# A decoder block on one core: the same program with its buffers at other places in SBUF

## The chip, the core and the metric

The kernel runs on one core of a Trainium2 chip. The core has TensorE (matrix products; called PE in the profile, its weight loads PEld), VectorE (DVE), ScalarE (ACT), GpSimd (POOL) and SyncE (SP), which issues the DMAs. They share an on-chip memory, SBUF, of 128 partitions; a buffer has the same byte range in every partition, and "place" below means the first byte of that range. Matrix products are written to another memory, PSUM. The metric is the time of one execution on the device in microseconds, the median over three executions.

## What is computed

One block of a decoder for 512 tokens of 1,024 features, in float32, with two attention branches and a feed-forward:

```python
xn = rmsnorm(x, norm_mix_g)
proj = xn @ w_in             # q_lat 384, kv_lat 256, k_rope 32, dq 512, dk 512, dv 512, gates 2048
# branch A: latent attention, 8 heads: q, k, v up-projected from the normed latents, rotary part shared by the heads
# branch B: differential attention, 4 heads: (softmax(q1 k1^T) - lam * softmax(q2 k2^T)) v, RMS norm per head
merged = sigmoid(g_mla) * (o_mla @ w_branch_mla) + sigmoid(g_diff) * (o_diff @ w_branch_diff)
x = x + merged @ w_out
hn = rmsnorm(x, norm_ffn_g)
hid = silu(hn @ w_ffn_gate) * (hn @ w_ffn_up)        # 2816 wide
x = x + hid @ w_ffn_down
return rmsnorm(x, norm_final_g)
```

## The kernel before

Every float32 operand of a product is split into a high and a low part (type float32r, `split` and `weights`), and `mm3` multiplies high by high, high by low and low by high into one PSUM bank: three matmuls, recorded on lines 297, 298 and 299. In the profile a matmul stands as `ps_mm<-X,w`: behind the arrow the first name is the operand that streams through TensorE, the second the stationary one, loaded ahead by a LDWEIGHTS. "128*128 128x512 f32" means 128x128 weights and 512 streamed columns, 2,048 bytes a partition.

The buffers come from one pool with tags; all buffers of a tag lie next to each other, and the tags lie in the order in which the program first asks for them. The tags that matter here:

- X: two buffers of 16 KB, the normed activations (features x tokens, both parts), first `xn`, later `hn`.
- w: three of 8 KB, split weights. They also take the first raw loads of the latents' weights.
- L: 22 of 4 KB, general tiles: inputs, queries, keys, values, branch outputs, the hidden activations, the residual.
- P: six of 2 KB, probabilities; PT: one of 10 KB, transposed probabilities, and later some other tiles.
- raw (weights as loaded), t (temporaries) and sm (columns of a few numbers), with some constants.

The program runs through these stages, which one can find by time in the profile: loads, norm and latents (to about 45 us); latent attention, with projections put between its parts (to about 190 us); differential attention with the gates between (to about 310 us); the branch products, where L streams past weights from w (to 355 us); the output projection (to 398 us); the feed-forward's gate and up products, where X streams past w (`ffn_product`; the first three products in halves of 256 columns, then 41 of 24 matmuls each); the down products, where w streams past the hidden tiles in L and PT (648 to 768 us); the final norm. Each gate and each projection of the differential attention's queries and keys also streams X past w, 24 matmuls of 512 columns each; its values and the latents use X as weights.

The order of instructions on each engine is fixed when the program is built. A block of weights comes by DMA into raw, ScalarE (or VectorE) makes the high part, VectorE (or GpSimd) the low part.

Of the kernel before, what the change touches and what calls it, by code (L numbers as in the profile page):

```python
# [21 lines left out]
P = 128  # L22
S = 512
# [69 lines left out]
def build(ctx, nc, tc, a, out):  # L93
# [9 lines left out]
    def T(tag, shape, dtype):  # L103
        return sb.tile(shape, dtype, name=nm(tag), tag=tag, bufs=BUFS[tag])
# [7 lines left out]
    def LF():  # L112
        return T("L", [P, 1024], F32)
# [12 lines left out]

    # Instructions of the attention go ahead of the products that fill the tensor engine around them.
    tc.cur_priority = 1000000
# [15 lines left out]

# [1 line left out]
    LOG_EXP = "natural_log_exp_and_others"  # L146
# [9 lines left out]

    # The tensor engine's clock rises after some microseconds of work: it gets some while the first loads run.
    warm = T("P", [P, S], BF16)
    nc.vector.memset(warm, 0.0)
    warm_ps = PS("pv")  # L160
    def dummies(n):
        for _ in range(n):
            nc.tensor.matmul(out=warm_ps, lhsT=warm[:, :P], rhs=warm, start=True, stop=True)
    xts = [LF() for _ in range(NB)]
    ones = sb.tile([P, P], F32, name="ones")
# [6 lines left out]
    misc = T("PT", [P, 2560], F32)  # L172
    lat_raw = [T("w", [P, 2, 1024], F32R) for _ in range(3)]

# [50 lines left out]

# [1 line left out]
    last_exp = [None]  # L227

    def rsqrt(ss, n, w=1):
        """1/sqrt(ss/n + eps), with one Newton step."""  # L230
        v, y, z = sm(w), sm(w), sm(w)
        nc.vector.tensor_scalar(out=v, in0=ss, scalar1=1.0 / n, scalar2=EPS, op0=ALU.mult, op1=ALU.add)
        log_exp(out=y, in_=v, func=AF.Ln)
        last_exp[0] = log_exp(out=y, in_=y, func=AF.Exp, scale=-0.5)
        if w == 1:
            nc.vector.tensor_scalar(out=z, in0=v, scalar1=y, scalar2=y, op0=ALU.mult, op1=ALU.mult)
        else:
            nc.vector.tensor_mul(out=z, in0=y, in1=y)
            nc.vector.tensor_mul(out=z, in0=z, in1=v)
        nc.vector.tensor_scalar(out=z, in0=z, scalar1=-0.5, scalar2=1.5, op0=ALU.mult, op1=ALU.add)  # L240
        nc.vector.tensor_mul(out=y, in0=y, in1=z)
        return y

    def split(src, hi, lo, scale=1.0):
        """src * scale = hi + lo, exactly, both with at most 12 significant bits."""
        if isinstance(scale, float):
            nc.scalar.activation(out=hi, in_=src, func=AF.Copy, scale=scale)  # L247
        else:
            nc.scalar.activation(out=hi, in_=src, func=AF.Identity, scale=scale)
        if isinstance(scale, float) and scale == 1.0:  # L250
            nc.vector.tensor_sub(out=lo, in0=src, in1=r32(hi))  # L251
        else:
            nc.vector.scalar_tensor_tensor(out=lo, in0=src, scalar=scale, in1=r32(hi),  # L253
                                           op0=ALU.mult, op1=ALU.subtract)
# [12 lines left out]
    def weights(src, n0, n1, pick=None):  # L267
        """Load a [128, n0, n1] block of weights (src: its parts along n0); returns its (hi, lo) parts. pick lists
        (heads, first, last): in that order, the columns first..last of each of the heads are kept."""
        raw = T("raw", [P, 1024], F32)  # L270
# [30 lines left out]
    def norm_transpose(xt, g, dst, t, junk):  # L301
        """RMS norm of 128 tokens, transposed to features x tokens, in two parts."""
        ss = sm()
# [13 lines left out]

# [1 line left out]
    xn = norm_tiles()  # L319
    last_t, last_hi = [None], [None]  # L320
# [11 lines left out]

    # The norm's 1 / rms is left out of xn: what is made of xn is scaled by it later.
    x_ss = sm(NB)

    def scaled_transpose(t0, t1):
        """Tokens times the norm's gains, transposed to features x tokens, in two parts."""
        n = t1 - t0
# [42 lines left out]
    nc.vector.tensor_mul(out=x_ms, in0=x_rs, in1=x_rs)  # L381
# [1 line left out]
    lp = lv[:, 0:4:2, :]  # L383
# [7 lines left out]

# [1 line left out]
    # Angle / 2 pi modulo 1: the angle in two parts and 1 / 2 pi in five, of 12 bits each, so that every product is  # L393
    # exact; whole turns are dropped product by product.
    nc.vector.tensor_copy(out=ang, in_=pos_i)
# [15 lines left out]
    for _ in range(2):  # L411
        nc.vector.tensor_scalar(out=ry[:, 0, :], in0=turn, scalar1=MAGIC, scalar2=0.0, op0=ALU.add, op1=ALU.add)
        nc.vector.tensor_scalar(out=ry[:, 0, :], in0=ry[:, 0, :], scalar1=MAGIC, scalar2=0.0, op0=ALU.subtract, op1=ALU.add)
        nc.vector.tensor_sub(out=turn, in0=turn, in1=ry[:, 0, :])
# [1 line left out]
    turn_c = ry[:, 1, :]  # L416
# [15 lines left out]
    load_log_exp(last_sin)  # L432
# [1 line left out]
    latn = [LF() for _ in range(NB)]  # L434
# [26 lines left out]

# [1 line left out]
    lat = []  # L463
# [9 lines left out]

# [1 line left out]
    gates, gate_tiles = {}, {}  # L475
# [11 lines left out]
    def sigmoids(after, bs):  # L487
        """All gates together, so that the scalar engine's tables change less often."""
        with tc.issue_after(after.ins):
            for b in bs:  # L490
                for m in range(KD):
                    last = nc.scalar.activation(out=gates[b, m], in_=gates[b, m], func=AF.Sigmoid,
                                                bias=col(R_BG + 8 * b + m), scale=1.0)
        load_log_exp(last)
# [23 lines left out]
    latent(1, 0, TAB_T)  # L518
    # 1 / rms of the tokens, the same on all partitions
    ps = PS("sc")  # L520
# [7 lines left out]

# [1 line left out]
    sel_r = T("P", [P, 4 * P], F32R)  # L530
# [38 lines left out]

# [1 line left out]
    def diff_project(c0):  # L571
# [8 lines left out]
    def diff_qk(h):  # L580
        """For each of the two maps, products of 128 rows (both parts of k, times the high part of q) and of 64 rows
        (the high part of k, times the low part of q)."""
        u = diff_project(C_DQ + h * P)
# [13 lines left out]

# [1 line left out]
    dv = []  # L599
# [14 lines left out]

# [1 line left out]
    def rope_key():  # L616
# [6 lines left out]

# [1 line left out]
    def scores(maps, i):  # L625
        """maps: (products (q, k) to add up, where). Softmax numerators of one block of 128 queries; returns 1 / their
        row sums."""
        n = (i + 1) * P
# [23 lines left out]
    def transposed(blocks):  # L652
        """Blocks of 128 queries x keys -> [keys, queries], in two parts, key block by key block."""
        pt = T("PT", [P, 2, 1280], F32R)
# [11 lines left out]
    def values(pt, v):  # L666
        """Sum over the keys of v(j, part), as [keys, 128], times pt."""
        ps = PS("pv")
# [5 lines left out]

# [1 line left out]
    ones_r = sb.tile([P, P], F32R, name="ones_r")  # L676
# [24 lines left out]
    def diff_norm(o32, sqs):  # L701
        """RMS norm over a head's 128 features, which lie on the partitions."""
        ps = PS("tr")
# [12 lines left out]

# [1 line left out]
    def mla_pe(g):  # L718
# [71 lines left out]
    def branch(b, m, o):  # L790
        """Gated branch output of 256 features, in place of the gates."""
        w = weights(kview(("w_branch_mla", "w_branch_diff")[b], m * P, 256), 4, 256)
# [7 lines left out]

# [1 line left out]
    mqk, pe, mv = {}, {}, {}  # L802
# [12 lines left out]

# [1 line left out]
    o_diff, parts = [], []  # L817
# [8 lines left out]

# [1 line left out]
    sigmoids(last_exp[0], (0, 1))  # L828
# [11 lines left out]

# [1 line left out]
    wo = {}  # L842
# [35 lines left out]

# [1 line left out]
    w_eng[:] = ["act", "dve"]  # L880
# [47 lines left out]
    def finish(t, c0, c1, ps):  # L928
        """Residual and final norm of some columns of 128 tokens; base: mean square of the columns so far, and eps."""
        xs = x1[t][:, c0:c1]  # L930
# [49 lines left out]
def _layout(inputs):  # L980
    """The inputs as the launch takes them: small ones gathered, positions repeated for 32 rows per block."""
    arrays = {n: np.ascontiguousarray(inputs[n]) for n in _INPUTS}
# [17 lines left out]
```

## Time and profile before

| | |
|---|---|
| median of three executions | 775.96 us (775.87 to 776.09) |
| span of the profiled execution, first to last instruction | 775.3 us |
| TensorE busy | 757.9 us, 98% of the span |
| VectorE, ScalarE, GpSimd busy | 429.7, 293.6, 166.8 us |
| mean granted TensorE clock | 0.996 of full speed |

The profile is of one execution; its span is 0.66 us shorter than the median time, which includes what lies before the first and behind the last instruction. Busy time of TensorE counts overlapping matmuls once, so it doesn't say how fast the matmuls follow each other; for that one reads start times, or counts matmuls in a stretch of time.

### The profile page before, as it was taken

What the parts mean: (1) busy time and instruction counts of PE and PEld (TensorE: products, weight loads), DVE (VectorE), ACT (ScalarE), POOL (GpSimd) and SP (SyncE); (2) the same over time, 40 slices, a digit from 0 to 9 for tenths busy, and PEclk for the clock granted to TensorE, in tenths of its full rate; (3) what the DMA queues carried; (4) which work ended last, traced back from release to release, by engine and by line L of the source; (5) the groups of instructions that cost most, each with busy time, mean ns of one, the idle gap of its engine ahead of it and who ended that gap; (6) DMA issues with size and microseconds to landing.
All of it is one profiled execution on the core that took longest, in us unless ns stands there. A gap on an engine that the chain in (4) does not pass through costs nothing.

```text
span 775.3 us, 9589 instructions
## 1 busy us (share of the span) xinstructions
PE 757.9 (98%) x3639; PEld 622.9 (80%) x3639; DVE 429.7 (55%) x800; ACT 293.6 (38%) x567; POOL 166.8 (22%) x120
## 2 busy tenths in 40 slices
PE   8999999999999999999999999999999999999996
PEld 6888999887676778888899888888888888888884
DVE  6869598888999873477454233333323332213424
ACT  7564667553434411724244232323222222212314
POOL 3405243664663444530000000000000000000302
PEclk9999999999999999999999999999999999999999
DMA  9405243523223222337222323323232322332302
GB/s 302 109 2 156 73 123 74 134 68 82 68 69 77 60 90 73 109 108 255 73 82 82 103 87 101 90 84 106 84 107 82 109 81 85 106 108 82 109 0 109
DMA packets 99180, 75.67 MB, mean 98 GB/s; under 512 B 6176, under 2 KB 86846, under 8 KB 99134
## 3 DMA queue, kind: packets, MB, share of 16 engines
q1 hardware_dynamic: 99133, 75.07, 32.7%
q8 instruction: 28, 0.46, 0.2%
q14 instruction: 19, 0.15, 0.1%
HBM read 69.81 MB, written 2.10 MB: 93 GB/s over the span
## 4 chain that ended last, share of the span: by engine, by line
PE 81%; DVE 12%; issue 2%; DMA 1%; ACT 1%; POOL 1%; SPq 1%; DVEq 0%; POOLq 0%; ACTq 0%
PE ps_mm L298 22%; PE ps_mm L297 22%; PE ps_mm L299 22%; PE ps_sc L634 2%; DVE L L253 1%; PE ps_sc L297 1%; PE ps_sc L298 1%; PE ps_tr L298 1%; PE ps_tr L297 1%; PE ps_tr L299 1%; PE ps_sc L299 1%; DVE L L251 1%; PE ps_tr L660 1%; DVE w L262 1%; DVE P L686 1%
## 5 line engine op out<-in xcount | busy, mean ns | idle before, releaser
L297 PE MATMUL ps_mm<-X,w 128*128 128x512 f32 (+1 forms) x568 | 221.1, 390 | 0.0
L298 PE MATMUL ps_mm<-X,w 128*128 128x512 f32 (+1 forms) x568 | 221.0, 389 | 0.0
L299 PE MATMUL ps_mm<-X,w 128*128 128x512 f32 (+1 forms) x568 | 220.4, 389 | 0.0
L265 DVE TENSOR_TENSOR w<-raw,w 128x1024 fp32r<-128x1024 f32 x66 | 82.3, 1248 | 164.7 <-ACT w L260 164.5
L260 ACT ACTIVATE w<-raw 128x1024 fp32r<-128x1024 f32 (+1 forms) x72 | 73.8, 1028 | 163.9 <-issue 82.4
L265 POOL TENSOR_TENSOR w<-raw,w 128x1024 fp32r<-128x1024 f32 (+3 forms) x48 | 102.4, 2135 | 119.4 <-DVE w L262 33.3
L298 PEld LDWEIGHTS ps_mm<-X,w 128*128 128x128 f32 x568 | 107.0, 188 | 23.8 <-issue 0.7
L297 PEld LDWEIGHTS ps_mm<-X,w 128*128 128x128 f32 x568 | 106.8, 188 | 24.0 <-issue 1.2
L299 PEld LDWEIGHTS ps_mm<-X,w 128*128 128x128 f32 x568 | 107.1, 189 | 23.7 <-issue 0.4
L935 POOL TENSOR_TENSOR L<-L,P 128x512 f32<-128x512 f32 (+1 forms) x9 | 11.6, 1298 | 417.4 <-ACT t L934 417.4
L155 ACT ACTIVATE P<-P,sm 128x128 f32<-128x128 f32 (+3 forms) x64 | 35.9, 560 | 62.0 <-DVE sm L638 61.8
L909 DVE TENSOR_TENSOR t<-t,ps_mm 128x512 f32<-128x512 f32 x22 | 15.1, 688 | 63.5 <-PE ps_mm L299 63.5
L634 PE MATMUL ps_sc<-L,L 96*128 96x128 f32 (+11 forms) x160 | 42.8, 349 | 2.9 <-DVE sm L638 2.9
L908 ACT ACTIVATE t<-ps_mm 128x512 f32<-128x512 f32 x22 | 13.1, 598 | 84.3 <-PE ps_mm L299 84.3
L634 PEld LDWEIGHTS ps_sc<-L,L 96*128 96x128 f32 (+2 forms) x160 | 27.0, 190 | 13.6 <-issue 6.3
L298 PE MATMUL ps_mm<-w,L 128*128 128x512 f32 (+1 forms) x100 | 37.2, 372 | 0.0
L297 PE MATMUL ps_mm<-w,L 128*128 128x512 f32 (+1 forms) x100 | 37.2, 374 | 0.0
L299 PE MATMUL ps_mm<-w,L 128*128 128x512 f32 (+1 forms) x100 | 37.1, 373 | 0.0
L262 DVE CAST w<-raw 128x1024 fp32r<-128x1024 f32 (+3 forms) x42 | 35.8, 851 | 2.0 <-PE ps_mm L299 1.4
L247 ACT ACTIVATE L<-t 64x512 fp32r<-64x512 f32 (+2 forms) x47 | 29.1, 624 | 16.9 <-POOL t L564 7.3
L298 PE MATMUL ps_mm<-L,w 128*128 128x512 f32 x90 | 35.4, 394 | 0.0
L251 DVE TENSOR_TENSOR L<-t,L 128x512 fp32r<-128x512 f32 (+2 forms) x37 | 33.2, 897 | 4.0 <-ACT L L247 3.6
(264 smaller groups left out, 1271.9 us busy)
## 6 DMA issues: line engine op xcount, KB each, us to landing
raw<-w_in SPq DMA_DIRECT2D x28, 512.0 KB, 4.0
raw<-w_ffn_gate SPq DMA_DIRECT2D x22, 512.0 KB, 3.8
raw<-w_ffn_up SPq DMA_DIRECT2D x22, 512.0 KB, 3.9
raw<-w_ffn_down SPq DMA_DIRECT2D x22, 512.0 KB, 3.6
raw<-w_out SPq DMA_DIRECT2D x8, 512.0 KB, 3.6
L<-L SPq DMA_DIRECT2D x24, 128.0 KB, 2.4
L<-x SPq DMA_DIRECT2D x8, 256.0 KB, 6.0
raw<-w_branch_mla SPq DMA_DIRECT2D x4, 512.0 KB, 3.4
```

Of the source, the lines that this page charges most:

```text
L155: return nc.scalar.activation(**kw)
L247: nc.scalar.activation(out=hi, in_=src, func=AF.Copy, scale=scale)
L251: nc.vector.tensor_sub(out=lo, in0=src, in1=r32(hi))
L260: nc.scalar.activation(out=o, in_=i, func=AF.Copy)
L262: nc.vector.tensor_copy(out=o, in_=i)
L265: (nc.vector if w_eng[1] == 'dve' else nc.gpsimd).tensor_sub(out=o, in0=i, in1=r32(hi))
L297: nc.tensor.matmul(out=o, lhsT=lh, rhs=rh, start=start, stop=False)
L298: nc.tensor.matmul(out=o, lhsT=lh, rhs=rl, start=False, stop=False)
L299: return nc.tensor.matmul(out=o, lhsT=ll, rhs=rh, start=False, stop=stop)
L634: nc.tensor.matmul(out=ps[:, :n], lhsT=q[:, i * P:n], rhs=k[:, 0:n], start=j == 0, stop=j == last)
L908: last_silu = nc.scalar.activation(out=g, in_=gate_ps, func=AF.Silu)
L909: nc.vector.tensor_mul(out=g, in0=g, in1=ps)
```

## The change

The program asks for its first X buffers, then the first w and L buffers, ahead of the first P buffer; the code that uses them is as it was. Comments are dropped too, which moves line numbers. The core of the diff:

```diff
+    xn = [T("X", [P, 4, 2, S], F32R) for _ in range(2)]
+    lat_raw = [T("w", [P, 2, 1024], F32R) for _ in range(3)]
+    xts = [LF() for _ in range(NB)]
...
     warm = T("P", [P, S], BF16)
     nc.vector.memset(warm, 0.0)
     warm_ps = PS("pv")
...
-    xts = [LF() for _ in range(NB)]
     ones = sb.tile([P, P], F32, name="ones")
     nc.vector.memset(ones, 1.0)
...
     misc = T("PT", [P, 2560], F32)
-    lat_raw = [T("w", [P, 2, 1024], F32R) for _ in range(3)]
...
-    xn = norm_tiles()
```

On every engine the same instructions stand in the same order with the same waits before and after, and the queue of DMAs is the same: only places differ. In bytes within a partition, and with the remainder of the first byte after division by 64:

```
buffers            before                remainder   after                 remainder
X    2 x 16384     155936 to 188704      32           16512 to  49280       0
w    3 x  8192     129664 to 154240       0           49280 to  73856       0
L   22 x  4096      28800 to 118912       0           73856 to 163968       0
P    6 x  2048      16512 to  28800       0          163968 to 176256       0
ones     512       118912 to 119424       0          176256 to 176768       0
PT   1 x 10240     119424 to 129664       0          176768 to 187008       0
ident    512       154400 to 154912      32          187168 to 187680      32
sm, t, tables, raw 188704 and up                     188704 and up, unchanged
```

## Rows read from the trace of the kernel before

**Rows 1.** The page: span; busy us, share and instructions of each engine.
```profile
span 775.3 us, 9589 instructions
...
PE 757.9 (98%) x3639; PEld 622.9 (80%) x3639; DVE 429.7 (55%) x800; ACT 293.6 (38%) x567; POOL 166.8 (22%) x120
```

**Rows 2.** Stretches: us, each engine's busy us (instructions), clock, DMA share, GB/s.
```profile
154.00:250.00 96.00, 93.21 (x414) 70.09 (x412) 88.98 (x177) 39.65 (x94) 53.06 (x30) 1.00 0.28 69
250.00:312.00 62.00, 62.00 (x276) 48.83 (x277) 40.46 (x75) 17.32 (x40) 28.36 (x14) 1.00 0.29 84
312.00:352.00 40.00, 40.00 (x178) 33.11 (x177) 26.48 (x40) 20.40 (x32) 14.90 (x7) 1.00 0.32 107
418.00:648.00 230.00, 230.00 (x984) 184.89 (x983) 76.22 (x82) 64.79 (x82) 0.00 (x0) 1.00 0.33 96
650.00:766.00 116.00, 116.00 (x513) 96.08 (x512) 34.85 (x44) 28.90 (x43) 9.21 (x7) 1.00 0.23 78
```

**Rows 3.** Chain that ended last, 154 to 250 us, share by line.
```profile
by line: issue 14.6%; DVE L L253 9.2%; DVE P L686 8.6%; DVE L L251 8.2%; DVE P L638 7.0%; DVE w L262 5.9%; POOL t L564 4.9%; DVE PT L251 4.8%; DVE P L687 4.3%; DVE t L561 3.8%; DVE t L562 2.7%; POOL w L265 2.6%; DVE L L485 2.3%; ACT P L155 
```

**Rows 4.** The same, 418 to 648 us, with its count of pieces.
```profile
by line: PE ps_mm L297 33.4%; PE ps_mm L298 33.4%; PE ps_mm L299 33.3%
982 pieces in order of time: start us, us, what
```

**Rows 5.** Groups by line and form: count, busy us, mean ns, idle before.
```profile
L297 PE MATMUL ps_mm<-X,w 128*128 128x512 f32 x520 | 208.0, 400 | 0.0
...
L298 PE MATMUL ps_mm<-L,w 128*128 128x512 f32 x90 | 35.4, 394 | 0.0
...
L297 PE MATMUL ps_mm<-w,L 128*128 128x512 f32 x84 | 32.6, 390 | 0.0
```

**Rows 6.** TensorE in order of time: start us, duration us; L streaming.
```profile
70.40 0.28 PE L299 MATMUL ps_mm<-w,L 128*128 128x256 f32 x1
...
70.76 0.28 PE L299 MATMUL ps_mm<-w,L 128*128 128x256 f32 x1
70.88 0.40 PE L297 MATMUL ps_mm<-L,w 128*128 128x512 f32 x1
...
72.27 0.39 PE L297 MATMUL ps_mm<-L,w 128*128 128x512 f32 x1
...
74.08 0.39 PE L299 MATMUL ps_mm<-L,w 128*128 128x512 f32 x1
```

**Rows 7.** Matmuls with X alone, by stretch: us, busy us, count, clock.
```profile
49.00:68.00 19.00, 11.45 (x47) 1.00 0.25 70
...
154.00:250.00 96.00, 70.41 (x268) 1.00 0.28 69
250.00:312.00 62.00, 50.11 (x200) 1.00 0.29 84
```

**Rows 8.** TensorE in order of time, X streaming 256 columns.
```profile
405.05 0.28 PE L299 MATMUL ps_mm<-X,w 128*128 128x256 f32 x1
...
406.83 0.28 PE L299 MATMUL ps_mm<-X,w 128*128 128x256 f32 x1
```

**Rows 9.** TensorE in order of time, around a wait for VectorE.
```profile
76.43 0.28 PE L297 MATMUL ps_mm<-w,X 128*128 128x256 f32 x1
78.07 0.79 PE L634 MATMUL ps_sc<-L,L 96*128 96x384 f32 x3 [1.36 <-DVE sm L638]
```

**Rows 10.** The same view, where the granted clock fell.
```profile
79.80:83.20 3.40, 3.40 (x17) 3.30 (x16) 1.54 (x7) 2.09 (x6) 0.67 (x2) 0.50 0.83 251
```

**Rows 11.** TensorE with PT: ns min/median/max, first and last start, forms.
```profile
L781 PE MATMUL ps_pv<-PT,L x64: 222/335/453, 92.3 to 188.7; 128*128 128x512 f32 x16, 128*128 128x384 f32 x16, 128*128 128x256 f32 x16, 128*128 128x128 f32 x16
L671 PE MATMUL ps_pv<-PT,L x48: 220/336/482, 213.7 to 297.9; 128*128 128x512 f32 x12, 128*128 128x384 f32 x12, 128*128 128x256 f32 x12, 128*128 128x128 f32 x12
```

**Rows 12.** TensorE in order of time, around two matmuls that stream P.
```profile
46.63 0.63 PE L537 MATMUL ps_tr<-P,P 128*128 128x512 f32 x2
47.10 0.29 PE L299 MATMUL ps_mm<-L,X 128*128 128x288 f32 x1
```

## The prediction, made before the change was timed

> **What bounds the kernel now.** I first read the totals of the page: the span is 775.3 us and TensorE is busy for 98% of it [rows 1]. I then read the busy time stage by stage [rows 2]. Between 154 and 250 us TensorE is busy for 93.21 of 96 us and VectorE for 88.98; the chain that ended last runs mostly over lines of VectorE there and names no line of TensorE among its largest shares [rows 3]. That is the one long stretch that TensorE doesn't set. In the other stretches shown TensorE has no free time at all. From 418 to 648 us, the feed-forward's gate and up products, the chain is TensorE alone, in 982 pieces of one matmul each [rows 4].
>
> A busy TensorE can still be a slow one, because a matmul's recorded duration overlaps the next one's start. What counts is the distance from start to start. A window counts each matmul that touches it, so two more than fit; I take two off. The reader is to see three numbers in [rows 2]. The feed-forward starts 982 matmuls in 230 us, one every 234.2 ns. The down products start 511 in 116 us, one every 227.0 ns. The branch products start 176 in 40 us, one every 227.3 ns. All of these are 128x128 times 128x512 in the same type, with the same split weights behind them. The durations agree: 400 ns on line 297 where X streams past weights from w, and 390 ns where w streams past weights from L [rows 5].
>
> What differs is the streamed operand. It is X in the feed-forward, w in the down products, L in the branches. In the branches w is the stationary operand, as it is in the feed-forward, so w isn't what is slow. A stream from L does start a little slow after other work: six starts from 70.88 to 72.27 us are 232 ns apart, and the eight from there to 74.08 us are 226 ns apart [rows 6]. X never gets there, in 982 matmuls with nothing between them. X is also unlike the others in its place: of the buffers that stream in these 512-wide products it is the highest, and its first byte, 155,936, is the only one of theirs that is not a multiple of 64. (The identity matrix, at 154,400, is off by the same 32 bytes, but streams only 128 columns in transposes, where nothing comparable stands beside it.)
>
> **What the change does, and its cost.** It adds and removes no instruction. Each engine has the same ones in the same order behind the same waits, and the DMAs are the same. Only starts move. X goes to 16,512, a multiple of 64 and now the lowest; w, L, P and PT keep their remainder of 0. So the question is what each matmul with X costs at its new place. No row shows X elsewhere, so I bound it. At worst it keeps 234.2 ns. At best it takes the 226.8 ns that lies between [rows 2]'s 227.0 and the 226 of [rows 6], a saving of 7.4 ns. I take the second, because L and w, whose streams are of the same size and type, both reach it, and their places share a remainder that X is about to get.
>
> There are 520 such matmuls on each of three lines, 1560 in all [rows 5]. I sum them by stretch.
> - Feed-forward, 418 to 648 us: 982 of them, nothing else on the chain. 982 x 7.4 ns = **7.3 us**. What could hide it is the weights' own preparation, but the down products take a block of weights per 24 matmuls as well, and run at 227.0 ns.
> - 250 to 312 us: 200 [rows 7], mixed with attention, TensorE never idle. After each interruption the first matmuls would be 232 ns apart as in [rows 6], a saving of 2.4 ns; later ones save 7.4. That is 0.5 to 1.5 us; runs are broken often but not always, so I take **1.0 us**.
> - 80 to 154 us: the rest, 1560 - 982 - 268 - 200 - 47 = 63, by the same bounds 0.15 to 0.47, I take **0.3 us**.
> - 154 to 250 us: 268 [rows 7], 0.6 to 2.0 us by the same bounds, but VectorE sets the end. I take **0**, the cover being VectorE's 88.98 busy us of 96. If this cover were thinner than it looks, up to 2.0 us come on top.
> - 49 to 68 us: 47 [rows 7], 0.1 to 0.35 us. Behind them TensorE starts one matmul at 76.43 us and the next at 78.07 us, after waiting 1.36 us for VectorE [rows 9]. Arriving earlier only lengthens this wait: **0**.
> - The opposite sign: the 144 half-wide matmuls with which the feed-forward begins (three products, two halves, 24 each). X's are 118.7 ns apart now (15 starts from 405.05 to 406.83 us [rows 8]), while L's go 120 ns apart (three from 70.40 to 70.76 us [rows 6]). If X takes the pace of the others, 144 x 1.3 ns = **0.2 us** are lost.
>
> The sum is 7.3 + 1.0 + 0.3 - 0.2 = 8.4 us. The profiled execution's span is 775.3 us and the median 775.96, so 0.66 us lie outside the span; I leave those as they are. 775.96 - 8.4 = 767.56, and I predict **767.5 us**.
>
> The clock could add or take a little. [...]
>
> [...] First the row: matmuls with X are 234.2 ns apart, those with w 227.0 [rows 2], and the places are what I can see to differ. [...]
>
> **The rivals.**
> 1. *Places make no difference.* Something else holds X back, or old and new starts are alike. Against it: same shape, same type, same lines, same roles as in the branches, and yet 7 ns. For it: no row shows the same buffer in two places. Time: 775.96 us, no change. [...]
> 2. *Height, not the remainder.* Buffers above some 152 KB would stream slowly. X gains as before, but the stretch that X leaves is then taken by P, PT and the last two of the 22 L buffers. PT streams in 64 + 48 matmuls of the attention [rows 11]; at 7.4 ns that is at most 0.8 us. The two L buffers hold an eleventh of the 270 streams of L past w (90 on each line [rows 5]): 0.2 us. VectorE's reads of P and PT between 154 and 250 us could suffer too; if half of its 88.98 us grew by 7.4 of 227 ns, 3.3%, that is 1.5 us. Taking the first two: 767.5 + 1.0 = 768.5 us, and 770.0 with the third. Against it: w's third buffer ends at 154,240, X begins at 155,936, and w is fast; the border would have to fall just between.
> 3. *The lowest bytes are a bad place* (the slower case). X's first 12 KB, three eighths of its columns, would lie where only P lay before. P streamed there in the rotary tables: two matmuls from 46.63 to 47.10 us take 235 ns each, start to start [rows 12], no better than X now. At 235 ns only five eighths of the 8.4 us are won, 5.2 us, and the time is 770.7 us. For a loss beyond the noise, the three eighths of the 1130 or so matmuls whose gain counts, 424, must eat 5.2 + 1.6 us: 16 ns each above today's 234, so 250 ns. At 250 ns or more the time is 777.5 us and up. Against it: rows 12 show 235, not 250, and those two stand between other work, where L's are slow as well [rows 6].
>
> **How the numbers follow.** A measurement of this kernel can tell about 0.2%, 1.55 us, from no change. My forecast gets 0.74, height 0.11, no difference 0.10, and the low place with its loss 0.03; 0.02 is left for the two ends of the clock. Faster by over 0.2%: 0.86, nearly all of the first two. Within 0.2%: 0.10. Slower: 0.04. The range: if all 1560 matmuls save 7.4 ns the time is 775.96 - 11.5 = 764.4, and a vanished half-clock stretch brings it to 762.7, which I think unlikely and cut at 763.5. Above, height with VectorE's share and the low place at 235 ns reach 770.0 and 770.7; I end at 770.5. That leaves out the no-change and slower cases, some 0.14, and the tails.
>
> **What would show each step.** In the profile after, the matmuls with X should be 389 or 390 ns long, and 418 to 648 us should hold some 1014 of them rather than 982. The down products should keep 227 ns; if those with PT or the high L buffers slow down, it is height. Spacing between 409 and 500 us that differs between the first tile of X and the second would speak for rival 3. VectorE's busy time between 154 and 250 us should stay, and TensorE's idle time there grow. The forecast is wrong if X's spacing stays at 234 ns, which would mean that neither height nor remainder is the cause, or if VectorE's stretch takes longer at the new places.

## The result and the profile after

The changed kernel takes 768.27 us (median of four executions: 767.03, 767.65, 768.89 and 1239.33; the last ran at a mean granted clock of 0.557 and is left out of the ratio). Beside it the kernel before took 776.03 us. The ratio is 0.9888 [0.9871, 0.9904]: 1.1% faster, where 767.5 us were predicted. The median of the three executions that count is 767.65 us, and the profiled one took the same.

The stretches after, with the columns of [rows 2]:

```profile
79.80:83.20 3.40, 3.40 (x28) 3.27 (x27) 2.09 (x7) 2.23 (x7) 0.48 (x1) 1.00 0.77 237
...
154.00:250.00 96.00, 92.36 (x411) 69.66 (x410) 88.49 (x177) 41.17 (x98) 52.06 (x29) 1.00 0.29 73
...
312.00:352.00 40.00, 40.00 (x178) 33.15 (x177) 28.36 (x44) 19.11 (x32) 12.34 (x5) 1.00 0.35 117
418.00:648.00 230.00, 230.00 (x1016) 190.44 (x1016) 77.46 (x83) 65.63 (x82) 0.00 (x0) 1.00 0.33 98
```

Between 418 and 648 us TensorE now touches 1016 matmuls, not 984. With two taken off, 1014 start in 230 us, one every 226.8 ns, against 234.2 before. X's products now end at 637.9 us, so the last ten us of this stretch belong to the down products, which have the same pace; the experiments below are compared over 440 to 630 us, where X alone streams. The branches, 178 in 40 us, are as they were. The granted clock between 79.8 and 83.2 us is 1.00 here and was 0.50 in [rows 10].

The first of X's three lines, as a group by line and form (columns of [rows 5]; the line numbers are three higher):

```profile
L300 PE MATMUL ps_mm<-X,w 128*128 128x512 f32 x520 | 204.5, 393 | 0.0
```

X's matmuls on this line went from a recorded 400 to 393 ns on average, those in attention included. Between 440 and 630 us alone the mean is 389 ns on each of the three lines, and was 396. The wait of [rows 9] stands in the same place:

```profile
76.11 0.28 PE L300 MATMUL ps_mm<-w,X 128*128 128x256 f32 x1
77.87 0.62 PE L636 MATMUL ps_sc<-L,L 96*128 96x384 f32 x2 [1.48 <-DVE sm L640]
```

Where the time came from is seen by following one and the same matmul through both traces. Its start before less its start after is what has been won up to there:

```
start before   start after   won so far   what lies just ahead
      49.65         49.54         0.11
      74.08         73.76         0.32    X streaming from 49 to 68 us
      78.07         77.87         0.20    the wait for VectorE
      90.29         88.56         1.73    the stretch at half the clock, before only
     130.72        129.01         1.71
     155.24        153.22         2.02    X streaming up to 155 us
     252.44        250.65         1.78    VectorE's stretch
     309.05        306.23         2.82    X streaming from 250 to 309 us
     398.70        395.89         2.81    branches and output projection: nothing
     414.82        412.19         2.62    half-wide products
     652.48        642.45        10.03    the feed-forward's 984 products
     766.72        756.69        10.03    down products: nothing
```

Of the 10.03 us between the two spans, 1.5 us are the clock's, and 8.5 us remain. The medians of the executions that count differ by 776.03 - 767.65 = 8.4 us. The spans differ by more than the times because the profiled execution of the kernel before, with 775.3 us, is longer than most: of 25 executions of that kernel timed beside run e1 below, 19 have spans of 773.9 to 774.3 us, which fits a stretch at half the clock that most don't have.

### The profile page after: what moved, and what is told of

It is laid out like the page before. It is cut to its first block, busy times and chain, and to the rows that moved or that the text cites. A ratio compares the mean times of both kernels' runs of the same rounds, so it can differ in the third digit from the quotient of the medians.

```text
span 765.3 us, 9589 instructions
## 1 busy us (share of the span) xinstructions
PE 747.1 (98%) x3639; PEld 620.6 (81%) x3639; DVE 429.9 (56%) x800; ACT 293.7 (38%) x567; POOL 167.0 (22%) x120
## 4 chain that ended last, share of the span: by engine, by line
PE 81%; DVE 12%; issue 3%; DMA 1%; ACT 1%; POOL 1%; SPq 1%; DVEq 0%; POOLq 0%; ACTq 0%
PE ps_mm L301 22%; PE ps_mm L300 22%; PE ps_mm L302 22%; PE ps_sc L636 2%; DVE L L256 1%; PE ps_sc L301 1%; PE ps_tr L301 1%; PE ps_sc L302 1%; PE ps_tr L300 1%; PE ps_tr L302 1%; PE ps_sc L300 1%; DVE L L254 1%; PE ps_tr L662 1%; DVE w L265 1%; DVE P L688 1%
## 5 line engine op out<-in xcount | busy, mean ns | idle before, releaser
L301 PE MATMUL ps_mm<-X,w 128*128 128x512 f32 (+1 forms) x568 | 217.9, 384 | 0.0
L300 PE MATMUL ps_mm<-X,w 128*128 128x512 f32 (+1 forms) x568 | 217.7, 384 | 0.0
L302 PE MATMUL ps_mm<-X,w 128*128 128x512 f32 (+1 forms) x568 | 217.3, 383 | 0.0
```

What stands on the lines that cost most here:

```text
L300: nc.tensor.matmul(out=o, lhsT=lh, rhs=rh, start=start, stop=False)
L301: nc.tensor.matmul(out=o, lhsT=lh, rhs=rl, start=False, stop=False)
L302: return nc.tensor.matmul(out=o, lhsT=ll, rhs=rh, start=False, stop=stop)
```

## The experiments

The prediction's reason was X's own first byte: 32 off a multiple of 64 before, on one after. Rivals were height and lowest place. A further one came up after the first four runs: that two places count together, since the change also set the *distance* between the streamed X and the stationary w to a multiple of 256 bytes (32,768; before, 26,272 = 102 x 256 + 160), and w and L were that far apart all along (100,864 = 394 x 256). The experiments insert unused bytes between buffers and change nothing else: instructions, order and waits are those of the kernel changed, except in h1 and where it is said. The table gives the places, the distance's remainder by 256, and how many matmuls touch 440 to 630 us, all with X, so that the spacing is 190 us divided by that number less two.

| kernel | X at | w at | X less w, modulo 256 | matmuls in 190 us | spacing, ns | median, us | ratio to before |
|---|---|---|---|---|---|---|---|
| before | 155,936 | 129,664 | 160 | 813 | 234.3 | 775.96 | 1 |
| after | 16,512 | 49,280 | 0 | 840 | 226.7 | 768.27 | 0.9888 [0.9871, 0.9904] |
| e1_high_0 | 155,968 | 129,664 | 192 | 816 | 233.4 | 775.32 | 0.9986 [0.9976, 0.9995] |
| e2_low_32 | 16,544 | 49,344 | 224 | 816 | 233.4 | 775.16 | 0.9986 [0.9976, 0.9997] |
| e4_low_64 | 16,576 | 49,408 | 192 | 816 | 233.4 | 774.51 | 0.9977 [0.9967, 0.9987] |
| e3_w_32 | 16,512 | 49,312 | 224 | 816 | 233.4 | 780.55 | 1.0053 [1.0034, 1.0072] |
| f1_all_32 | 16,544 | 49,312 | 0 | 840 | 226.7 | 768.65 | 0.9908 [0.9887, 0.993] |
| f2_high_96 | 156,032 | 129,664 | 0 | 840 | 226.7 | 768.19 | 0.9905 [0.9885, 0.9925] |
| f3_d128 | 16,640 | 49,792 | 128 | 816 | 233.4 | 774.82 | 0.9983 [0.9974, 0.9993] |
| f4_d16 | 16,528 | 50,304 | 16 | 822 | 231.7 | 774.02 | 0.9968 [0.9955, 0.9981] |

**Height and remainder: e1, e2, e4.** The first starts from the kernel before, the others from the changed one.

```diff
# e1_high_0 (before): X 32 bytes higher, all behind it where 64 put it
+    pad0 = sb.tile([P, 8], F32, name="pad0")
     xn = norm_tiles()
+    pad1 = sb.tile([P, 8], F32, name="pad1")
# e2_low_32 (after); e4_low_64 has 16 floats twice
+    pad0 = sb.tile([P, 8], F32, name="pad0")
     xn = [T("X", [P, 4, 2, S], F32R) for _ in range(2)]
+    pad1 = sb.tile([P, 8], F32, name="pad1")
```

> The kernel before, with 32 bytes left free below X and 32 above it: X begins at 155,968, still the highest of the streamed buffers, but now a multiple of 64. Nothing else changes its remainder. If the remainder of X's start is the cause, X's matmuls go 226.7 ns apart, 418 to 648 us hold some 1016 of them, and the time is about 767.6 us, as for the changed kernel. If height is the cause, they stay 234 ns apart (984) and the time stays at 776 us.

> The changed kernel, with 32 bytes left free below X and 32 above it: X begins at 16,544, the lowest, 32 past a multiple of 64, and all others keep a remainder of 0. If the remainder is the cause, X's matmuls go back to 234 ns and the time to 776 us, though X lies low. If height is the cause, they stay at 226.7 ns and the time at about 767.6 us.

> The changed kernel, with 64 bytes left free below X and 64 above it: X begins at 16,576, a multiple of 64 but not of 128, as the changed kernel's 16,512 is. If a multiple of 64 is enough, nothing changes: about 767.6 us and 226.7 ns. If a multiple of 128 is what counts, X's matmuls go to 230 ns or more and the time rises by 3 to 8 us.

All three stay slow. The stretch of the feed-forward in e1:

```profile
440.00:630.00 190.00, 190.00 (x816) 153.08 (x815) 63.62 (x68) 52.86 (x68) 0.00 (x0) 1.00 0.32 94
```

and in e4:

```profile
440.00:630.00 190.00, 190.00 (x816) 153.10 (x815) 63.63 (x68) 52.75 (x69) 0.00 (x0) 1.00 0.32 94
```

X high with remainder 0 is slow, and X low with remainder 0 (e4) is as slow, 233.4 ns both times. So neither height nor X's remainder by 64 is the cause; my reason falls, and the rival of height with it.

**The other partner, e3.** X stays where the change put it; w moves 32 bytes.

```diff
     xn = [T("X", [P, 4, 2, S], F32R) for _ in range(2)]
+    pad0 = sb.tile([P, 8], F32, name="pad0")
     lat_raw = [T("w", [P, 2, 1024], F32R) for _ in range(3)]
+    pad1 = sb.tile([P, 8], F32, name="pad1")
     xts = [LF() for _ in range(NB)]
```

> The changed kernel, with 32 bytes left free below w and 32 above it: w begins at 49,312, remainder 32; X keeps 0. If any streamed operand is slowed by this remainder, the 528 down products, which stream w, go from 226.7 to 234.3 ns: 4.0 us, so about 771.6 us, while the feed-forward, where w is only the stationary operand, keeps 226.7. If stationary operands count too, the feed-forward falls back as well and the time is 779 us or more. If X alone is concerned (its shape, its writers), nothing changes: 767.6 us.

```profile
312.00:352.00 40.00, 40.00 (x173) 32.15 (x172) 26.47 (x41) 19.14 (x31) 13.38 (x6) 1.00 0.34 109
440.00:630.00 190.00, 190.00 (x816) 153.10 (x815) 63.62 (x68) 53.24 (x68) 0.00 (x0) 1.00 0.32 94
660.00:756.00 96.00, 96.00 (x413) 77.31 (x412) 27.29 (x28) 21.87 (x28) 5.89 (x4) 1.00 0.24 77
```

The second and the third stretch in the changed kernel, whose row of the first stands in the section on the result (178 matmuls):

```profile
440.00:630.00 190.00, 190.00 (x840) 157.30 (x839) 65.53 (x70) 54.30 (x69) 0.00 (x0) 1.00 0.33 97
660.00:756.00 96.00, 96.00 (x425) 79.48 (x424) 30.50 (x41) 25.76 (x40) 9.25 (x7) 1.00 0.21 72
```

X hasn't moved and is slow again. The branches, where L streams past w, and the down products, where w streams past L, have for the first time become slow too: in the branches 171 starts in 40 us are 233.9 ns apart, 176 are 227.3, and in the down products 411 starts in 96 us are 233.6 ns apart, 423 are 227.0. That makes e3 slower than the kernel before, 780.55 against 775.92 us. Products are slow whether w streams or stands still, so it looks as if the pair counts; that it isn't w's new place by itself is shown by f1, where w begins at the same 49,312 bytes and the feed-forward goes at 226.7 ns.

**The pair apart from the places, f1 to f4.** f1 shifts everything by 32 bytes, so that X has its old remainder and the pair still agrees. f2 starts from the kernel before and makes the pair agree by 96 bytes below X, with X still highest. f3 and f4 take the distances 128 and 16.

```diff
# f1_all_32 (after)
+    pad0 = sb.tile([P, 8], F32, name="pad0")
     xn = [T("X", [P, 4, 2, S], F32R) for _ in range(2)]
# f2_high_96 (before)
+    pad0 = sb.tile([P, 24], F32, name="pad0")
     xn = norm_tiles()
+    pad1 = sb.tile([P, 8], F32, name="pad1")
# f3_d128 (after): 32 floats below X, 96 behind it
# f4_d16 (after): X begins 16 bytes into a buffer that is 512 bytes longer
+        return T("X", [P, 4096 + 128], F32R)[:, 4:4100].rearrange("p (k s n) -> p k s n", k=4, s=2)
```

> The changed kernel, with 32 bytes left free below X and none above: X begins at 16,544 as in the run with X alone moved by 32, but w, L, P and PT (and all that lies above) move by the same 32 bytes. The four runs so far fit neither height nor the remainder of X's own start; they fit a theory of the pair: a matmul is slow when the starts of its streamed and its stationary operand differ by something that is not a multiple of 128. By that theory X and w agree here: 226.7 ns, and about 767.6 us. If a remainder of X's own start by 128 is what counts, X stays at 233 ns and w and L become slow too: 780 us or more.

> The kernel before, with 96 bytes left free below X and 32 above it: X begins at 156,032, the highest of the streamed buffers, 26,368 above w, 206 times 128. By the theory of the pair X's matmuls take 226.7 ns, and this alone gives the whole gain: about 767.6 us. By height they stay at 234 ns: 776 us. If the pair must agree by 512 bytes and not 128, they stay slow as well, since 26,368 is 256 over a multiple of 512.

> The changed kernel, with 128 bytes left free below X and 384 above it: X begins at 16,640, w at 49,792; the two differ by 128 over a multiple of 512 (and of 256), while the other pairs are as in the changed kernel. If the pair must agree by 128, nothing changes: 226.7 ns, about 767.6 us. If by 256 or 512, X's matmuls take 233 ns or more: 775 us.

> The changed kernel, with each X buffer widened by 512 bytes and X's data beginning 16 bytes into it: X begins at 16,528, 16 over a multiple of 128 apart from w, and all other pairs agree. By the theory of the pair this is slow as well: 233 to 236 ns for X, 774 to 778 us. If only differences of 32 bytes and more count, 226.7 ns and 767.6 us.

The feed-forward in f1:

```profile
440.00:630.00 190.00, 190.00 (x840) 157.44 (x839) 65.56 (x71) 54.23 (x69) 0.00 (x0) 1.00 0.33 97
```

in f2:

```profile
440.00:630.00 190.00, 190.00 (x840) 157.42 (x839) 64.84 (x69) 54.68 (x70) 0.00 (x0) 1.00 0.33 96
```

in f3:

```profile
440.00:630.00 190.00, 190.00 (x816) 152.91 (x815) 63.60 (x68) 52.71 (x69) 0.00 (x0) 1.00 0.32 94
```

and in f4:

```profile
440.00:630.00 190.00, 190.00 (x822) 154.35 (x821) 63.64 (x68) 54.14 (x70) 0.00 (x0) 1.00 0.32 94
```

f1 and f2 have the whole gain, 226.7 ns, with X in the two places that should have been wrong for it: at the old remainder, and at the top. f2's distance is 103 x 256, so 512 isn't asked for; f3's 233.4 ns show that 128, the theory until then, isn't enough. From here on "agree" means that the first bytes differ by a multiple of 256. A distance of 16 costs 5.0 ns per matmul, less than expected, the others that don't agree 6.7 to 7.6.

**One pair of three, g1.** In the changed kernel the low part of each block of weights starts 32 bytes later; two of `mm3`'s three matmuls use the high part and agree still.

```diff
-        w = T("w", [P, 2, 1024], F32R)
+        wt = T("w", [P, 2112], F32R)
+        w = [wt[:, 0:1024], wt[:, 1032:2056]]
```

> The changed kernel, with the low part of each split weight block begun 32 bytes later than its place, the high part and all other buffers agreeing by 256 bytes. Of the three matmuls of a product in the feed-forward, the first and second then have stationary weights that agree with X, the third has weights that don't. If a matmul's own stationary operand counts, the start of the third delays what follows it: the distance behind the third grows to 231 to 236 ns. If it is the weights that are loaded while it streams (the next matmul's), the distance behind the second grows instead. Either way the mean of the three is about 229 ns and the feed-forward 2 to 3 us longer; in the down products, where w streams and L stands, only the second, which streams the low part, should be slow. About 771 us. If one agreeing pair in three is not enough to be fast, all three go to 233 ns and the time is 776 to 779 us.

```profile
312.00:352.00 40.00, 40.00 (x173) 32.14 (x172) 25.89 (x40) 19.90 (x32) 14.65 (x7) 1.00 0.32 107
440.00:630.00 190.00, 190.00 (x816) 152.74 (x815) 63.57 (x68) 53.26 (x68) 0.00 (x0) 1.00 0.32 94
660.00:756.00 96.00, 96.00 (x416) 77.70 (x415) 27.15 (x28) 22.51 (x28) 5.90 (x4) 1.00 0.24 79
```

The feed-forward has the slow mean, 233.4 ns, though only one matmul in three disagrees, and the kernel takes 779.04 us, a ratio of 1.0038 [1.0024, 1.0053], where about 771 us were expected. The branches, with 171 starts in 40 us, 233.9 ns each, and the down products, with 414 in 96 us, 231.9 ns, are slow too. The three lines between 440 and 630 us (first, second and third matmul of a product are 301, 302 and 303):

```profile
L302 PE MATMUL ps_mm<-X,w 128*128 128x512 f32 x272 | 108.8, 400 | 0.0
L301 PE MATMUL ps_mm<-X,w 128*128 128x512 f32 x272 | 107.4, 395 | 0.0
L303 PE MATMUL ps_mm<-X,w 128*128 128x512 f32 x272 | 105.8, 389 | 0.0
```

From start to start it is 232 ns behind the first of the three, 239 behind the second, 229 behind the third, and the recorded durations have the same order. The longest distance lies behind the second, which agrees, and not behind the third, which doesn't: the weights of the third are loaded while the second streams (read in the kernel before, where line 299's load, 0.19 us long, and line 298's matmul both start at 440.36 us).

**Narrow products, g2.** The first byte of ident (128 columns stream in each transpose) stood 160 bytes over a multiple of 256 from those of P and L. It is made to agree, by 24 and 40 floats ahead of and behind it:

> The changed kernel, with 96 bytes left free below the identity matrix and 160 above the mask: ident now begins a multiple of 256 apart from P and L. It streams only 128 columns, in some 220 transposes that are 109 ns apart. If pairs matter there as well, each is a little faster, 0.5 us in all at most, since most lie where others set the end; otherwise nothing: 767.6 us, and 109 ns. X's matmuls keep 226.7 ns.

768.69 us, 0.9904 [0.9889, 0.9918], like the changed kernel; transposes that follow each other start 109.9 ns apart on average, 109.7 in the changed kernel. With 128 columns nothing was won.

**The product's own weights or the next one's, h1.** In the feed-forward the first four slices of each block agree with X and the last four start 32 bytes later: twelve matmuls that agree, then twelve that don't. (The expectation speaks of two instructions for each split; the edit makes one instruction over both halves, and the counts of all engines are as in the changed kernel.)

```diff
+        w = T("w", [P, 2112], F32R)[:, :2064].rearrange("p (h x) -> p h x", h=2)
+        rv = raw.rearrange("p (h x) -> p h x", h=2)
+        round_hi(w[:, :, 0:512], rv)
+        round_lo(w[:, :, 512:1024], rv, w[:, :, 0:512])
```

> Made from the changed kernel: of each block of FFN weights the first four slices stand as before, and the last four start 32 bytes later, so that the FFN goes through twelve products whose two operands agree modulo 256 bytes, then twelve whose operands stand 32 bytes apart, and so on. The weight splits take two instructions of half the width in place of one. Theory A (the product's own two places count): the first product of a run that disagrees is already long, the last one that agrees is short; a run that agrees goes back to 226.7 ns after six to nine products, so the mean lies between 227 and 233 ns and the time between 769 and 774 us. Theory B (the weights that are loaded for the next product while this one streams count): the last agreeing product of a run is long already, and the last disagreeing one short; the time is the same as with A. Theory C (a run of twelve is too short to settle): 233 ns throughout, 775 to 776 us, and A and B aren't told apart.

It takes 771.24 us, 0.9931 [0.991, 0.9953]:

```profile
440.00:630.00 190.00, 190.00 (x827) 154.88 (x826) 63.97 (x69) 53.15 (x68) 0.00 (x0) 1.00 0.32 95
```

TensorE's matmuls and weight loads in order of time, about the change from agreeing to not (the matmul of 506.18 us is the last that agrees):

```profile
506.18 0.40 PE L311 MATMUL ps_mm<-X,w 128*128 128x512 f32 x1
506.18 0.19 PEld L309 LDWEIGHTS ps_mm<-X,w 128*128 128x128 f32 x1
506.41 0.39 PE L309 MATMUL ps_mm<-X,w 128*128 128x512 f32 x1
```

While the last agreeing matmul, of line 311, streams, the weights of the next one, line 309, are loaded; these are the first that disagree. The mean distance to the next start, in ns, for each place in the 24, over 39 of the blocks between 420 and 645 us:

```
 1 230.8    7 226.7   13 230.8   19 235.0
 2 226.7    8 226.7   14 229.2   20 231.7
 3 226.6    9 226.6   15 235.0   21 235.0
 4 226.7   10 226.7   16 231.6   22 231.7
 5 226.7   11 226.7   17 235.0   23 235.0
 6 226.6   12 235.0   18 231.7   24 232.5
```

The twelfth agrees in itself and is the first long one, 235 ns in each of the 39 blocks. So the entry is as theory B has it, by which the weights that are being loaded for the next product count against the operand that streams, and theory A, which has the thirteenth as the first long one, falls as it was put down. The recorded durations agree: 397 ns for the twelfth, 389 for the ten ahead of it, while the weight load keeps 187 to 188 ns. One other reading isn't excluded: that a product whose own two places disagree starts late. X streams in the twelfth and in the thirteenth, so the starts alone can't tell the two apart, and the recorded ends of matmuls are modelled. At the exit B alone doesn't hold: the 24th should be short by it and has 232.5 ns, and one more, the first, has 230.8. In place of the expected six to nine agreeing products until the pace settles, there was one. In the half that disagrees, long and shorter ones take turns, a pattern that no theory of mine gives.

## Why the prediction was right, and where its reason was wrong

**The number.** 767.5 us were predicted and 767.65 measured. The sum by its terms, beside the trace:

| term | predicted, us | measured, us |
|---|---|---|
| feed-forward, 982 matmuls | 7.3 | 7.4 |
| 250 to 312 us | 1.0 | 1.04 |
| 80 to 154 us | 0.3 | 0.31 |
| 154 to 250 us | 0 | -0.24 |
| 49 to 68 us | 0 | 0.20 |
| half-wide products | -0.2 | -0.19 |
| sum | 8.4 | 8.5 |
| the stretch at half the clock | not in the sum | 1.5 |

Taking L's and w's pace for X's at its new place was right to within 0.1 ns. VectorE's stretch hid X's gain as said: VectorE's busy time stayed (88.49 us after) and TensorE's idle time there grew from 2.79 to 3.64 us. The wait of [rows 9] was expected to swallow all of the 0.32 us that had been won ahead of it. It swallowed 0.12, growing from 1.36 to 1.48 us, and the matmul behind it starts 0.20 us earlier; what let VectorE release it earlier was not looked at. The half-wide products took on the others' 120 ns, and so lost what was said:

```profile
402.03 0.28 PE L300 MATMUL ps_mm<-X,w 128*128 128x256 f32 x1
...
404.43 0.28 PE L302 MATMUL ps_mm<-X,w 128*128 128x256 f32 x1
```

That is 20 starts in 2.40 us, 120 ns each, against 118.7 in [rows 8].

Three readings in the working were off and left the sum as it was. The 0.66 us outside the span compare the span of one execution with the median of others: every execution whose span is on record took 1.7 to 3.0 us longer than its own span. So the profiled 775.3 us belong to a time above the median, and a vanished stretch at half the clock could give the median of 775.96 us little, since most executions of the kernel before, as their spans go, were without it. The 1.7 us that the range takes off for it at its lower end, from 764.4 to 762.7, are shown by no run; between the two traces the stretch made 1.5 us. The durations in [rows 5], 400 against 390 ns, show one of X's three lines over all stages; in the feed-forward X's mean was 396. And the 1014 matmuls expected between 418 and 648 us can't all be X's, of which the feed-forward has 984 of this width; 971 of those that start there now are.

**The reason.** The step that failed is the one that chose between the two bounds: "because L and w, whose streams are of the same size and type, both reach it, and their places share a remainder that X is about to get." X's remainder isn't it: with its old remainder X is fast (f1, 226.7 ns), and with the remainder that it was "about to get" it is slow (e1, e3, e4 and f3, 233.4 ns). In the kernel before L and w agreed *with each other*, and I read this as a property of each: the sentence that w "isn't what is slow", because it stands still in the branches as well, looks at one operand at a time. The change brought X into step with w by its new order, in which whole buffers of 16 KB lie between the first byte of X and that of w; 32 more bytes between them (e3) gave no gain but a loss, 780.55 us. The price and the pace were read from rows and held. The cause was argued from a coincidence of places, so that this change hit the fast pace by luck as far as the stated reason goes, and the prediction listed no rival in which two places count together. Nor did it look at the places of the partners, which were all known before the run.

**The rivals.** That places make no difference falls with the result: in the ten kernels of the table the two places together set the pace, 226.7 ns where they agree and 231.7 to 234.3 where they don't. Height falls by f2, which is as fast with X on top as the changed kernel, 226.7 ns. The lowest place as a bad one falls by the change itself: of the 983 distances between X's products of the feed-forward, 978 are 226 or 227 ns, which leaves no room for a slower part of X.

**What stays open.** What it is about two places that don't agree that costs the 5.0 to 7.6 ns is shown by no run. Nor does one tell whether the long product is held up by the weights that are loaded during it, or the next one starts late by its own two places. Why 16 bytes cost less than 32 (5.0 ns in f4, 6.7 in e3), and why two products in h1, the 24th and the first (232.5 and 230.8 ns), are still slow when no disagreeing weights are loaded any more, is not settled.

## What to carry to other kernels

Where a profile shows back-to-back 512-column products whose starts are some 3% further apart than those of like products, look at the places of both operands of each product, not of one: let every buffer that streams and every buffer of weights start a multiple of 256 bytes apart, as 96 unused bytes below X and 32 above it did here for the whole gain (f2, 226.7 ns against 234.3). Parts of a buffer have to keep that step too, as g1 and h1 show (233.4 and 230.3 ns on average); in the feed-forward of the changed kernel they do. Other types and shapes were not tried, except that narrower products gained nothing (with 256 columns 120 ns after and 118.7 before, with 128 columns 109.9 in g2 and 109.7 in the changed kernel). Check after each change of the allocation that pairs which agreed still do, since a shift of 32 bytes cost the changed kernel 1.5 to 1.7% (g1 and e3, 779.04 and 780.55 against 767.65 us). And count starts in a stretch; a 98% busy TensorE hid this.

## What the hardware showed that I had not expected

- 512-column float32r products whose two operands agree modulo 256 bytes start 226.7 ns apart, those that don't 231.7 to 234.3, in the ten kernels of the table without an exception; neither X's place nor w's sorts them by itself.
- One disagreeing block of weights in three matmuls is enough to slow all three (g1, 229 to 239 ns), and the distance that grows first is the one ahead of the matmul that disagrees (h1, 235 ns where the ten ahead of it have 226.6 or 226.7).
- With 256 columns the sign turned: 118.7 ns where the pair disagreed, 120 where it agrees. All runs bear this out: over the half-wide products with X the mean distance (those under 140 ns) is 119.7 to 119.8 ns in the four profiles where the pair agrees throughout (the changed kernel, f1, f2, g2) and 115.7 to 118.8 in the others.
- The stretch at half the clock near 80 us [rows 10] came and went: five of the thirteen profiles had it (a mean granted clock of 0.60 to 0.70 between 80 and 84 us, and 1.00 in the other eight), among them ones with X high (before) and low (g1), so that a single profiled pair can differ by 1.5 us of luck.
